# Cutting the token groups of a z product from 272, 384 and 384 columns to 272, 256, 256 and 256, with one 64-column product ahead of the first 256

## The chip, the cores and the metric

The kernel runs on one core of a Trainium2 chip, in one launch. Times are device microseconds (us). The time before is the median of three runs, 1241.5 us (1241.24 to 1242.45). A core has a matrix engine (PE, with its weight loads listed apart as PEld), a vector engine (DVE), a scalar engine (ACT), a general engine (POOL) and a queue engine (SP) that issues most transfers. Each engine works through its own list of instructions in order; semaphores tie the lists together. PE writes its sums only to PSUM, a small memory of eight banks, from which ACT or DVE must read ("evacuate") a sum before its buffer can be used again.

## The reference

One layer of a decoder over 1040 tokens (16 meta tokens and 1024 of the sequence), width 1024, float32:

```
z = h @ w_in + b_in                                  # 1024 -> 3840 columns
q, k, v, c_in, gates = split(z)                      # 512, 128, 128, 2*512, 2*1024
y_attn = sliding_window_attention(q, k, v) @ w_attn_proj
c = c_val * sigmoid(c_gate);  c = causal_dwconv(c, 31 taps)
y_conv = silu(layer_norm(c)) @ w_conv_proj
mixed = sigmoid(g_attn) * y_attn + sigmoid(g_conv) * y_conv
h = layer_norm(alpha * h + mixed @ w_out)
h = layer_norm(alpha * h + conv_ffn(h))              # 1024 -> 2*2816 -> 1024
```

The change touches the first line and the two projections that make y_attn and y_conv.

## The kernel before, in words

**Products in three terms.** Every operand of a large product is split into a high part and a low part. `product` (L294) forms, for each of eight blocks of 128 rows, high times high (L298), high times low (L302) and low times high (L303), all summed into one PSUM bank. The weights are the stationary operand (128 x 128, loaded by a LDWEIGHTS of its own ahead of each product); the tokens are the moving operand, with as many columns as the group has tokens.

**The z product.** z is computed in 30 tiles of 128 output columns. The first three (k, v and the first of q) are computed at the start, between the transposes that make h (L509 and L512), in groups `HG` = 272, 384 and 384 tokens (L54); the change leaves their groups alone. The other 27 go through `z_tile` (L313) and `z_group` (L306): for each token group a PSUM tile `ps_z` is taken from a ring of three buffers (tag "mm"), 24 products are issued, and the group's evacuation follows. Eight tiles belong to the convolution (`conv_chunk`, L640: a gate tile evacuated by ACT, L646, then a value tile evacuated by DVE into `cin`, L654, and then 31 taps on DVE over 1026 tokens, L661 and L663), three to q (evacuated by ACT at L350, with a split on DVE, L353), sixteen to the merge gates (`gate_tile`, ACT, L670, each followed by a store to `sgd` that ACT's queue issues). The q and gate tiles use `TG`, whose first group has 258 tokens in place of 272.

**Where h lies.** h0 (L255) gives the slice of h, high or low, of one block and token range; h lies in two arrays, RHO and RHC, group after group. ACT's evacuations go to staging slots in FA: `stage` (L325), five slots of 400.

**The order of work.** Each instruction has a rank; a scheduler, which simulates the engines when the kernel is built, writes each engine's list. Evacuations rank ahead of most work. While PE works on z, DVE works through the residual rows (L445), the taps, the attention's softmax, and the layer norm of the convolution; the attention's small products (scores `ps_s` L834, transposes `ps_t` L870, values `ps_o` L883) are scattered among the z products. The first product of the two meta queries is held back to a given product of the first gate tile (`ahead`).

**The projections.** After z come eight column tiles of the two projections (`branch`, from L1122): four groups `PG` of 258, 256, 256 and 256 tokens, and in each group twelve products with the attention output (OA) and twelve with the convolution (OC), into `ps_p`. After them come the product with w_out (`ps_w`), the up projection (L1552, tokens in halves of 258 and 256) and the down projection (L1696, 512 columns).

Of the kernel before, what the change touches and what calls it, by code (L numbers as in the profile page):

```python
# [31 lines left out]
KC = D // P  # L32
# [3 lines left out]
U0 = 14  # L36
# [17 lines left out]
HG = [(0, 272), (272, 656), (656, 1040)]  # L54
UG = [(0, 258), (258, 642), (642, 1026)]

PG = [(0, 258), (258, 514), (514, 770), (770, 1026)]


HW = 514  # L60
# [40 lines left out]
def tile_hybrid_layer(  # L101
# [3 lines left out]
    nc = tc.nc  # L105
# [36 lines left out]
    FA = arena.tile([P, 6144], F, name="FA")  # L142
    RHC = arena.tile([P, 8320], R, name="RHC")
    RHO = arena.tile([P, 8320], R, name="RHO")
# [22 lines left out]
    start = ExitStack()  # L167
# [85 lines left out]


    def h0(k, hl, a, b):  # L255
        g = next(g for g, x in enumerate(HG) if a < x[1])
        x, y = HG[g]
        i, n = (k % 4) * 2 + hl, y - x
        o = i * n + ((6144 if i else 0), 272, 3344)[g]
        return (RHO if k < 4 else RHC)[:, o + a - x:o + b - x]  # L260


    tc.cur_priority = RK_QKV
# [27 lines left out]

    chunks_done = []

    def product(ps, terms, behind=None):  # L294

        n = len(terms)
        for i, (ah, al, bh, bl) in enumerate(terms):
            ins = nc.tensor.matmul(ps, ah, bh, start=i == 0, stop=False)  # L298
            chunks_done.append(ins)
            if i == 0 and behind is not None:  # L300
                after(ins, behind)
            nc.tensor.matmul(ps, ah, bl, start=False, stop=False)  # L302
            last = nc.tensor.matmul(ps, al, bh, start=False, stop=i == n - 1)  # L303
        return last

    def z_group(wt, g, a, b, evac):  # L306
        hi, lo = wt
        ps = pat.tile([P, 512], F, name="ps_z", tag="mm", bufs=3)
        product(ps[:, :b - a], [(hi[:, k], lo[:, k], h0(k, 0, a, b), h0(k, 1, a, b)) for k in range(KC)])
        with rank(RK_EVAC):  # L310
            evac(g, a, b, ps[:, :b - a])

    def z_tile(fill, groups, evac, wt=None):  # L313
        wt = wt or weights([P, KC, P], fill)
        for g, (a, b) in enumerate(groups):
            z_group(wt, g, a, b, evac)

    def in_cols(m):
        return lambda raw: load(raw, w_z[m])

    TG = [(a + U0 if i == 0 else a, b) for i, (a, b) in enumerate(HG)]

    st_next = [0]

    def stage(n, lo=4104, cnt=5):  # L325
        i = st_next[0] % cnt
        st_next[0] += 1
        return FA[:, lo + i * 400:lo + i * 400 + n]

    tc.cur_priority = RK_QKV + 1000  # L330

# [272 lines left out]
    for a, b in ((0, 400), (400, J_LEN)):  # L604
        ps = pat.tile([P, 512], F, name="ps_v", tag="o" if a == 0 else "t", bufs=1 if a == 0 else 2)
# [5 lines left out]
    wt_c1 = [weights([P, KC, P], in_cols(m)) for m in (11, 7)]  # L611
# [28 lines left out]
    def conv_chunk(c):  # L640
        sig = {}

        def g_evac(g, a, b, ps):
            sig[g] = stage(b - a)

            nc.scalar.activation(sig[g], ps, AF.Tanh, bias=bcol(10 + c), scale=0.5)  # L646
            nc.scalar.activation(sig[g], sig[g], AF.Identity, bias=half_, scale=0.5)

        z_tile(in_cols(10 + c), HG, g_evac, wt_c1[0] if c == 1 else None)
        cin = cp.tile([P, 16 + T], F, name="cin", tag="cin")  # L650
        nc.vector.memset(cin[:, 0:16], 0.0)

        def v_evac2(g, a, b, ps):
            nc.vector.scalar_tensor_tensor(cin[:, 16 + a:16 + b], ps, bcol(6 + c), sig[g], OP.add, OP.mult)  # L654

        z_tile(in_cols(6 + c), HG, v_evac2, wt_c1[1] if c == 1 else None)
        with rank(RK_CONV + c * 100):
            for j in range(TAPS):
                wc = cdw[:, j * CH + c:j * CH + c + 1]
                if j == 0:  # L660
                    nc.vector.tensor_scalar(acc[c], cin[:, j:j + U], wc, cdwb(c), OP.mult, OP.add)  # L661
                else:
                    nc.vector.scalar_tensor_tensor(acc[c], cin[:, j:j + U], wc, acc[c], OP.mult, OP.add)  # L663
# [38 lines left out]
    ps = pat.tile([P, 512], F, name="ps_vm", tag="t", bufs=2)  # L702
# [4 lines left out]
    for q4 in range(2):  # L707
        ps = pat.tile([P, 512], F, name="ps_v4", tag="t", bufs=2)
        for i in range(4):
            c = NMETA + (q4 * 4 + i) * P  # L710
# [30 lines left out]
    tc.cur_priority = RK_Z - 500  # L741
    first_chunk = len(chunks_done)
    gate_tile(0)
    ahead = chunks_done[first_chunk + 2 * KC + 5]

    tc.cur_priority = RK_ATT

# [255 lines left out]
    def oo(r, hl, a, b):  # L1003
        return OA[:, place(r * 2 + hl, a, b)]
# [114 lines left out]
    for m in range(KC):  # L1119
        hi, lo = weights([P, KC, P], lambda raw: load(raw, w_ab[m]))  # L1120

        def branch(i, g, tag, bufs):  # L1122
            a, b = PG[g]
            ps = pat.tile([P, 512], F, name="ps_p", tag=tag, bufs=bufs)
            rhs = (oo, conv)[i]
            product(ps[:, :b - a], [(hi[:, 4 * i + k], lo[:, 4 * i + k], rhs(k, 0, a, b), rhs(k, 1, a, b))
                                    for k in range(4)])
            return ps[:, :b - a]

        def merge(g, psa, psb):  # L1130
            a, b = PG[g]
            n = b - a
            with rank(RK_EVAC):
                t = gslot()[:, :, :n]
                ins = load(t, dram(sgd, m * P * U + a, [[U, P], [KC * P * U, 2], [1, n]]))

                ta, tb = t[:, 0], t[:, 1]
                nc.vector.scalar_tensor_tensor(ta, ta, 1.0, psa, OP.add, OP.mult)
                nc.vector.scalar_tensor_tensor(tb, tb, 1.0, psb, OP.add, OP.mult)
                nc.vector.tensor_tensor(ta, ta, tb, OP.add)  # L1140
                if g == 0:
                    nc.scalar.mul(pair[:, m, 0:2], ta[:, 0:2], 0.5)
                v = ta[:, n - 256:].rearrange("p (t x) -> p t x", t=2)
                h = mixed2(g, m, 0)
                last_act = nc.scalar.mul(h, v, 0.5)
                nc.vector.scalar_tensor_tensor(mixed2(g, m, 1), v, 0.5, f32(h), OP.mult, OP.subtract)
            return ins, last_act

        if m < KC - 1:
            for g in range(4):  # L1150
                last_gate, last_act = merge(g, branch(0, g, "mm", 3), branch(1, g, "t", 2))
        else:
            pa = [branch(0, g, "mm", 3) if g < 3 else branch(0, g, "s", 2) for g in range(4)]
            for g in range(4):
                last_gate, last_act = merge(g, pa[g], branch(1, g, "t", 2))
        if m in (2, 3):
            raw = (FA[:, 4112:5136], OB[:, 3072:4096])[m - 2]
            load(raw, w_out_v[m + 2])
            prep_wo(m + 2, raw, last_act)
        if m < 4:  # L1160
            early.append(FA[:, W_AT[m]:W_AT[m] + 1024])
            wo_raw[m] = early[m]
            after(load(early[m], w_out_v[m]), last_gate)
        if m > 1:
            with rank(RK_PROJ + 3000):
                two_rows(m - 2)
# [261 lines left out]
    ahead = []  # L1428
# [422 lines left out]
```

## Time and profile before

| what | value |
|---|---|
| median of three runs | 1241.5 us (1241.24 to 1242.45) |
| the profiled execution | 1241.26 us, of which the span is 1239.5 us |
| granted clock of the profiled execution | 0.998 |
| z tiles of the three-group loop | PE from 56.5 to 408.0 us of the span |
| projections | PE from 408.0 to about 503 us |
| DVE busy, whole span | 1084.0 us (87%) |
| ACT busy, whole span | 580.0 us (47%) |

The span runs from the first to the last instruction that the profile shows; the execution's time has 1.76 us around it. A row of the timeline gives the start in us from the span's start, the duration in us, the engine, the line, the operation, output and inputs, their shape and count, and in brackets an idle time ahead of it with what ended it. Matmuls overlap: a row's duration is longer than the distance to the next row, and their ends are modelled. So the time that a product costs a full PE is read as the distance between starts.

### The profile page before, as it was taken

To read this page: it belongs to the slowest core of one execution; us is meant where nothing else is said; L and a number is where in the kernel's file an instruction comes from. 1 tells how busy PE (TensorE), PEld (TensorE's weight loads), DVE (VectorE), ACT (ScalarE), POOL (GpSimd) and SP (SyncE) were. 2 spreads that over 40 slices of the span, in tenths; PEclk is the share of its full clock that TensorE was granted. 3 is DMA by queue.
4 is the path that set the end of the run, shared out by engine and by line. 5 is a ranking of instruction groups with operands and counts; after the bars stand their busy time and mean duration, and the time that the engine had idled before them with its cause. 6 is when DMAs were issued, how large, how long until landed. Compare 5 with 4: busy or idle time off the path is not lost.

```text
span 1239.5 us, 21702 instructions
## 1 busy us (share of the span) xinstructions
PE 1229.4 (99%) x8540; PEld 1170.7 (94%) x8540; DVE 1084.0 (87%) x1846; ACT 580.0 (47%) x1047; POOL 12.7 (1%) x11
## 2 busy tenths in 40 slices
PE   9999999999999999999999999999999999999997
PEld 8999999999999999888999999999999998888885
DVE  7899989999978798659899999998999986995697
ACT  7532336654255323344755555455454454544330
POOL 0000000000000010000000000000000000000000
PEclk9999999999999999999999999999999999999999
DMA  7287844412255554222145555544455469987722
GB/s 283 67 300 152 199 115 107 132 37 90 75 164 154 168 165 140 102 87 85 52 171 203 205 179 213 182 176 153 162 203 194 176 239 319 391 320 290 255 85 85
DMA packets 109024, 213.08 MB, mean 172 GB/s; under 512 B 31739, under 2 KB 48683, under 8 KB 108794
## 3 DMA queue, kind: packets, MB, share of 16 engines
q1 hardware_dynamic: 93002, 200.63, 49.1%
q10 hardware_dynamic: 15920, 11.07, 2.9%
q8 instruction: 67, 1.10, 0.4%
q14 instruction: 35, 0.29, 0.1%
HBM read 150.04 MB, written 62.70 MB: 172 GB/s over the span
## 4 chain that ended last, share of the span: by engine, by line
PE 98%; DVE 1%; ACT 0%; issue 0%; DVEq 0%
PE px L1552 14%; PE py L1552 9%; PE ps_x L1696 9%; PE ps_z L302 8%; PE ps_z L298 8%; PE ps_z L303 8%; PE ps_z L1696 7%; PE pw L1552 5%; PE pz L1552 5%; PE ps_p L298 2%; PE ps_p L303 2%; PE ps_p L302 2%; PE ps_w L303 2%; PE ps_w L298 2%; PE ps_w L302 2%; PE ps_z L512 2%
## 5 line engine op out<-in xcount | busy, mean ns | idle before, releaser
L663 DVE SCALAR_TENSOR_TENSOR FA<-cin,cols,FA 128x1026 f32<-128x1026 f32 x120 | 152.1, 1278 | 0.9
L303 PE MATMUL ps_z<-RHO,wlo 128*128 128x384 f32 (+2 forms) x324 | 104.1, 321 | 0.0
L298 PE MATMUL ps_z<-RHO,whi 128*128 128x384 f32 (+2 forms) x324 | 103.9, 321 | 0.0
L302 PE MATMUL ps_z<-RHO,whi 128*128 128x384 f32 (+2 forms) x324 | 103.9, 321 | 0.0
L303 PE MATMUL ps_z<-RHC,wlo 128*128 128x384 f32 (+2 forms) x324 | 103.8, 320 | 0.0
L302 PE MATMUL ps_z<-RHC,whi 128*128 128x384 f32 (+2 forms) x324 | 103.7, 320 | 0.0
L298 PE MATMUL ps_z<-RHC,whi 128*128 128x384 f32 (+2 forms) x324 | 103.6, 320 | 0.0
L269 ACT CAST whi<-wr 128x1024 fp32r<-128x1024 f32 x37 | 38.9, 1051 | 88.7 <-PE ps_z L302 69.2
L1361 ACT CAST RHO<-wr 128x512 fp32r<-128x512 f32 x92 | 55.3, 619 | 26.2 <-DMA wr<-in_w_up_dram 12.3
L1362 DVE TENSOR_TENSOR RHO<-wr,RHO 128x512 fp32r<-128x512 f32 x92 | 61.9, 684 | 5.3 <-ACT RHO L1361 5.3
L298 PEld LDWEIGHTS ps_z<-RHO,whi 128*128 128x128 f32 x324 | 61.0, 188 | 0.1
L298 PEld LDWEIGHTS ps_z<-RHC,whi 128*128 128x128 f32 x324 | 61.1, 189 | 0.0
L303 PEld LDWEIGHTS ps_z<-RHO,wlo 128*128 128x128 f32 x324 | 61.0, 188 | 0.0
L302 PEld LDWEIGHTS ps_z<-RHO,whi 128*128 128x128 f32 x324 | 61.0, 188 | 0.0
L302 PEld LDWEIGHTS ps_z<-RHC,whi 128*128 128x128 f32 x324 | 61.0, 188 | 0.0
L303 PEld LDWEIGHTS ps_z<-RHC,wlo 128*128 128x128 f32 x324 | 60.9, 188 | 0.0
L1379 DVE TENSOR_TENSOR wr<-wr 128x512 f32<-128x512 f32 x88 | 60.1, 683 | 0.2
L272 DVE TENSOR_TENSOR wlo<-wr,whi 128x1024 fp32r<-128x1024 f32 x35 | 42.6, 1218 | 11.2 <-ACT whi L269 11.1
L670 ACT ACTIVATE FA<-ps_z,cols 128x384 f32<-128x384 f32 (+1 forms) x48 | 26.1, 543 | 47.7 <-PE ps_z L303 39.8
L1564 ACT COPY FA<-px 128x514 f32<-128x514 f32 (+2 forms) x23 | 13.1, 571 | 72.3 <-PE px L1552 72.2
L1361 ACT CAST ws<-wr 128x512 fp32r<-128x512 f32 x60 | 36.1, 618 | 17.0 <-DVE wr L1379 10.7
L1552 PE MATMUL px<-OA,RHO 128*128 128x258 f32 (+1 forms) x336 | 43.9, 279 | 0.0
(466 smaller groups left out, 3478.0 us busy)
## 6 DMA issues: line engine op xcount, KB each, us to landing
wr<-in_w_up_dram SPq DMA_DIRECT2D x44, 512.0 KB, 4.5
wr<-in_w_z_dram SPq DMA_DIRECT2D x30, 512.0 KB, 4.1
fd<-FA SPq DMA_DIRECT2D x44, 256.0 KB, 2.4
OB<-in_w_down_dram SPq DMA_DIRECT2D x19, 512.0 KB
qt<-qd SPq DMA_DIRECT2D x28, 256.0 KB, 4.2
sgd<-FA ACTq DMA_DIRECT2D x32, 192.0 KB, 3.0
td<-OB SPq DMA_DIRECT2D x12, 512.0 KB
sums<-fd SPq DMA_DIRECT2D x12, 512.0 KB, 7.0
```

Of the source, the lines that this page charges most:

```text
L269: ins = nc.scalar.copy(hi, raw)
L272: return (nc.vector if quick else nc.gpsimd).tensor_tensor(lo, raw, f32(hi), OP.subtract)
L298: ins = nc.tensor.matmul(ps, ah, bh, start=i == 0, stop=False)
L302: nc.tensor.matmul(ps, ah, bl, start=False, stop=False)
L303: last = nc.tensor.matmul(ps, al, bh, start=False, stop=i == n - 1)
L663: nc.vector.scalar_tensor_tensor(acc[c], cin[:, j:j + U], wc, acc[c], OP.mult, OP.add)
L670: nc.scalar.activation(t, ps, AF.Tanh, bias=bcol(14 + i), scale=0.5)
L1361: nc.scalar.copy(hi, src)
L1362: ins = nc.vector.tensor_tensor(lo, src, f32(hi), OP.subtract)
L1379: ins = nc.vector.tensor_tensor(*x)
L1552: ins = nc.tensor.matmul(o, x[:, ks], bmat(sub, q, hl, k), start=first and k + j == 0, stop=k == 3 and j == 2, skip_group_check=not first)
L1696: nc.tensor.matmul(banks[i], l[:, ts], r[:, ws], start=first and a and x + k == 0, stop=z and x == len(ops) - 1 and k == 2, skip_group_che ...
```

## The change

It gives the 27 z tiles of `z_tile` four groups (`ZG` = 272, 256, 256, 256; with 258 as the first for q and the gates) in place of three. In each of these tiles, ahead of the first group of 256, `product` issues one more product of 64 columns with the first block's high weights into the same PSUM tile; the next product starts the sum afresh and overwrites it. The same is done once in each of the eight column tiles of the projections, whose groups stay as they were. h is laid out anew, so that tokens 272 to 1040 of a block lie in one piece. The staging slots become seven of 286 for small groups; the five of 400 remain for the first q tile. `ahead` counts eight blocks more, so that it names the same place of the gate tile.

```diff
 PG = [(0, 258), (258, 514), (514, 770), (770, 1026)]
+ZG = [(0, 272), (272, 528), (528, 784), (784, 1040)]
...
     def h0(k, hl, a, b):
-        g = next(g for g, x in enumerate(HG) if a < x[1])
-        x, y = HG[g]
-        i, n = (k % 4) * 2 + hl, y - x
-        o = i * n + ((6144 if i else 0), 272, 3344)[g]
-        return (RHO if k < 4 else RHC)[:, o + a - x:o + b - x]
+        i = (k % 4) * 2 + hl
+        if a < 272:
+            o = i * 272 + (6144 if i > 2 else 0)
+        else:
+            o = 816 + i * 768 - 272
+        return (RHO if k < 4 else RHC)[:, o + a:o + b]
...
-    def product(ps, terms, behind=None):
+    def product(ps, terms, behind=None, lead=None):

         n = len(terms)
+        if lead is not None:
+            nc.tensor.matmul(ps[:, :64], terms[0][0], lead, start=True, stop=True)
         for i, (ah, al, bh, bl) in enumerate(terms):
...
     def z_group(wt, g, a, b, evac):
         hi, lo = wt
         ps = pat.tile([P, 512], F, name="ps_z", tag="mm", bufs=3)
-        product(ps[:, :b - a], [(hi[:, k], lo[:, k], h0(k, 0, a, b), h0(k, 1, a, b)) for k in range(KC)])
+        product(ps[:, :b - a], [(hi[:, k], lo[:, k], h0(k, 0, a, b), h0(k, 1, a, b)) for k in range(KC)],
+                lead=h0(0, 0, 0, 64) if g == 1 else None)
...
-    TG = [(a + U0 if i == 0 else a, b) for i, (a, b) in enumerate(HG)]
-
-    st_next = [0]
-
-    def stage(n, lo=4104, cnt=5):
-        i = st_next[0] % cnt
-        st_next[0] += 1
-        return FA[:, lo + i * 400:lo + i * 400 + n]
+    TG = [(a + U0 if i == 0 else a, b) for i, (a, b) in enumerate(ZG)]
+
+    st_next = [0, 0]
+
+    def stage(n):
+        big = n > 272
+        cnt, size = ((7, 286), (5, 400))[big]
+        o = 4136 + st_next[big] % cnt * size
+        st_next[big] += 1
+        return FA[:, o:o + n]
...
-        z_tile(in_cols(10 + c), HG, g_evac, wt_c1[0] if c == 1 else None)
+        z_tile(in_cols(10 + c), ZG, g_evac, wt_c1[0] if c == 1 else None)
...
-        z_tile(in_cols(6 + c), HG, v_evac2, wt_c1[1] if c == 1 else None)
+        z_tile(in_cols(6 + c), ZG, v_evac2, wt_c1[1] if c == 1 else None)
...
-    ahead = chunks_done[first_chunk + 2 * KC + 5]
+    ahead = chunks_done[first_chunk + 2 * KC + 5 + KC]
...
             product(ps[:, :b - a], [(hi[:, 4 * i + k], lo[:, 4 * i + k], rhs(k, 0, a, b), rhs(k, 1, a, b))
-                                    for k in range(4)])
+                                    for k in range(4)],
+                    lead=oo(0, 0, 0, 64) if i == 0 and g == 1 else None)
             return ps[:, :b - a]
```

## The prediction, made before the changed kernel was run

> **What bounds the kernel now.** I read the page's head and chain first, then the groups of PE instructions with their shapes, then the busy time by stage, and at last PE's timeline in the stages that the change touches.
>
> ```profile
> span 1239.5 us, 21702 instructions
> PE 1229.4 (99%) x8540; PEld 1170.7 (94%) x8540; DVE 1084.0 (87%) x1846; ACT 580.0 (47%) x1047; POOL 12.7 (1%) x11
> PE 98%; DVE 1%; ACT 0%; issue 0%; DVEq 0%
> ```
>
> PE is busy for 99% of the span and makes 98% of the chain that ends last. So what counts is the time for which each product holds PE. But DVE is close behind:
>
> ```profile
> 56.50:136.50 80.00, 80.00 (x515) 79.92 (x515) 76.28 (x91) 24.15 (x43) 0.00 (x0) 1.00 0.77 206
> 136.50:316.30 179.80, 179.80 (x1272) 178.80 (x1271) 169.94 (x352) 89.16 (x250) 0.00 (x0) 1.00 0.40 108
> 316.30:408.00 91.70, 91.70 (x590) 91.70 (x589) 77.19 (x132) 42.69 (x66) 0.00 (x0) 1.00 0.49 144
> ```
>
> The columns are the stretch, its length, and the busy time of PE, PEld, DVE, ACT and POOL, then PE's granted clock. The three stretches are z: first q and convolution tiles, then tiles with the attention among them, then gate tiles. DVE is busy for 95% of the first two. PE never sits idle, so a gain must come from cheaper products, and every wait that the change brings PE is lost in full.
>
> **What a product costs.** Durations overlap, so I take distances between starts.
>
> ```profile
> 327.54 0.28 PE L298 MATMUL ps_z<-RHO,whi 128*128 128x258 f32 x1
> 330.44 0.34 PE L298 MATMUL ps_z<-RHO,whi 128*128 128x384 f32 x1
> 338.76 0.28 PE L298 MATMUL ps_z<-RHO,whi 128*128 128x258 f32 x1
> ```
>
> This is one undisturbed gate tile: 24 products of 258 columns in 2.90 us (0.121 each), 48 of 384 in 8.32 us (0.1733 each), 11.22 us in all. The 256-column product occurs in the projections, in runs of 60 to 72, at two paces:
>
> ```profile
> 433.36 0.28 PE L298 MATMUL ps_p<-OA,whi 128*128 128x256 f32 x1
> 440.43 0.28 PE L298 MATMUL ps_p<-OA,whi 128*128 128x258 f32 x1
> ...
> 422.29 0.29 PE L298 MATMUL ps_p<-OA,whi 128*128 128x256 f32 x1
> 429.10 0.28 PE L298 MATMUL ps_p<-OA,whi 128*128 128x258 f32 x1
> ```
>
> The run at 433.36 takes 7.07 us for 60, or 0.1178 each; the one at 422.29 takes 6.81 us, or 0.1135 each. In the projections two runs (422.29 and 456.09) are fast and six slow. The up projection is fast nearly throughout:
>
> ```profile
> 821.45 1.52 PE L1552 MATMUL py<-OC,RHO 128*128 128x256 f32 x12
> 822.81 1.41 PE L1552 MATMUL px<-OA,RHO 128*128 128x256 f32 x11
> ```
>
> Twelve in 1.36 us are 0.1133 each. Three groups of 256 replace two of 384: 72 products at 0.1133 are 8.16 us against 8.32, a gain of 0.16 per tile; at 0.1178 they are 8.48, a loss of 0.16. So the pace decides the sign. What sets it? One place shows a run that follows short products:
>
> ```profile
> 597.90 0.60 PE L1331 MATMUL py<-cols,OB 128*128 128x128 f32 x4
> 598.34 0.60 PE L1331 MATMUL pz<-cols,OB 128*128 128x128 f32 x4
> 598.69 1.64 PE L1552 MATMUL pw<-RHC,RHO 128*128 128x256 f32 x12
> 600.16 1.61 PE L1552 MATMUL py<-OC,RHO 128*128 128x256 f32 x12
> 601.61 0.28 PE L1552 MATMUL px<-RHC,RHO 128*128 128x256 f32 x1
> ```
>
> Four transposes of 128 columns take 0.44 us, 0.11 each: with so few columns the spacing is no longer set by columns, but (I take it) by the weight load. From 598.34 to 600.16, four of them and twelve products of 256 take 1.82 us. Less 0.44 that is 1.38, which is twelve fast products and 0.02 for falling into step. The next twelve, after a short hitch at 600.16, take 1.45 us, or 0.1208, hitch included: slow again. So a run entered from a short product goes fast, and a small wait makes it slow. A 64-column product is such a short one; I take it that the lead does what it is placed for, from this one instance.
>
> **The change part by part.**
>
> *The lead.* Nearest row to it is a single product of 8 columns among products of 384:
>
> ```profile
> 182.40 0.34 PE L302 MATMUL ps_z<-RHO,whi 128*128 128x384 f32 x1
> 182.58 0.17 PE L798 MATMUL ps_o<-p,va 80*128 80x8 f32 x1
> 182.61 0.43 PE L303 MATMUL ps_z<-RHO,wlo 128*128 128x384 f32 x1
> 182.88 0.33 PE L298 MATMUL ps_z<-RHO,whi 128*128 128x384 f32 x1
> ```
>
> Two products of 384 and the small one take 0.48 us; less 0.347 the small one costs 0.13. Bounds: 0.11 (a transpose) and 0.15 (this with 0.02 for falling into step). I take 0.13. There are 27 leads in z and 8 in the projections.
>
> *An undisturbed tile* then takes 2.90 + 0.13 + 8.16 = 11.19 us, a gain of 0.03. Over 27 tiles: **-0.8**.
>
> *Tiles with the attention among them.* Twelve tiles lie between 136.5 and 316.3. In the built order of the changed kernel 58 stretches of 256 begin behind an attention product. A stretch of 256 pays 0.02 to fall into step, one of 384 about 0.01:
>
> ```profile
> 178.58 1.04 PE L790 MATMUL ps_t<-cols,s 128*16 128x128 f32 x8
> 179.63 0.34 PE L298 MATMUL ps_z<-RHO,whi 128*128 128x384 f32 x1
> ```
>
> (1.05 us for eight transposes at 0.109 and one product of 384 at 0.173.) So 58 x 0.01 = **+0.6**, bounds 0 and 1.2. And some stretches will be slow, since most begin behind transposes or scores but some behind a wait or the 256-column `ps_o`. All twelve slow would cost 12 x 72 x 0.0045 = 3.9; none, nothing. I take a quarter: **+1.0**.
>
> *A new wait at the second tile.* A tile now takes four turns of the three PSUM buffers, so its last group needs the buffer of its first. In the value tile of conv chunk 1 that buffer is read late:
>
> ```profile
> 68.38 0.29 PE L298 MATMUL ps_z<-RHO,whi 128*128 128x272 f32 x1
> 71.37 0.34 PE L298 MATMUL ps_z<-RHO,whi 128*128 128x384 f32 x1
> ...
> 74.34 1.21 DVE L272 TENSOR_TENSOR wlo<-wr,whi 128x1024 fp32r<-128x1024 f32 x1
> 75.47 2.34 DVE L445 TENSOR_TENSOR OB<-OB,gb 128x1024 f32<-128x1024 f32 x2
> 77.75 1.01 DVE L654 SCALAR_TENSOR_TENSOR cin<-ps_z,cols,FA 128x272 f32<-128x272 f32 x2
> ...
> 79.70 0.29 PE L298 MATMUL ps_z<-RHO,whi 128*128 128x272 f32 x1
> ```
>
> DVE runs without a gap up to the evacuation at 77.75 and frees the buffer at about 78.2. Before, its next user starts at 79.70. In the built order DVE has the same instructions ahead of that evacuation, so 78.2 stays. PE now reaches the fourth group at 71.37 + 0.13 + 48 x 0.1133 = 76.9, and waits 1.3, with the wake-up **+1.4**. Behind it on PE stands everything. Bounds: 0 (if DVE gets there earlier) and 1.4.
>
> *Evacuations.*
>
> ```profile
> L654 DVE SCALAR_TENSOR_TENSOR cin<-ps_z,cols,FA 128x384 f32<-128x384 f32 x8 | 4.9, 611 | 2.3 <-PE ps_z L303 2.3
> L670 ACT ACTIVATE FA<-ps_z,cols 128x384 f32<-128x384 f32 x16 | 9.2, 578 | 17.9 <-PE ps_z L303 10.1 <-DMA sgd<-FA 7.4 <-ACT FA L670 0.5
> ...
> 346.63 0.33 ACTq L116 DMA_DIRECT2D sgd<-FA  x1
> ```
>
> A tile has one more, estimated at three of some 465 ns for two of about 600. On DVE that is some 0.2 in each of the four value tiles and as much for the splits of three q tiles; on ACT, with 0.33 for the issue of one more store, some 0.5 in each of the others. Stores of the gates and writes of q grow in number by a third, not in bytes. All this lies beside PE, and I cost it at nothing. It has cover as long as attention operands come early: in
>
> ```profile
> 200.62 0.69 DVE L874 TENSOR_TENSOR pl<-ps_t,ph 80x512 fp32r<-80x512 f32 x1
> 205.01 0.28 PE L883 MATMUL ps_o<-pl,va 80*128 80x256 f32 x1
> ```
>
> DVE ends 3.7 us ahead of PE's use. The built order puts fewer taps and fewer z products ahead of each attention step, by my sums of the rows' durations up to 5 us less for DVE than for PE; the margin and the wait above take that up. Without them PE would wait 1 to 2 us more.
>
> *Projections.* Six of eight runs are slow, 348 products in all (72, four of 60, 36). At 0.0043 that is -1.5; eight leads cost +1.04. Together **-0.5**.
>
> *The new layout of h* moves no work: the same slices are written and read.
>
> **Sum:** -0.8 + 0.6 + 1.0 + 1.4 - 0.5 = +1.7. On the profiled execution's 1241.26 us (span 1239.5 and 1.76 around it) that is 1242.96; the median of the runs lies 0.24 higher, so **1243.2 us**. Faster or slower is what differs by over 0.2%, 2.5 us, which is about what a measurement can tell from no change.
>
> **The rivals.**
>
> *The pace is not to be had in z (slower).* Products of 258 and 384 lie on a line: 0.0523 us for 126 columns, so 0.107 for 258 and a fixed 0.014. By it 256 columns cost 0.120, and the measured 0.1178 is near. If the lead doesn't help, or a first wait undoes it, each z tile takes 2.90 + 0.13 + 8.48 = 11.51, +0.29, 7.8 for 27; the projections' eight leads and the loss of the two quick stretches (132 x 0.0043) give +1.6; the wait is then 1.1. In all +10.5: 1252. It decides as soon as some three z tiles more than I count run slow (0.32 each, past the 2.5 us). Against it stand the fast up projection and the run behind the transposes. The Trainium skill speaks for it too: TensorE: Matmul & The Clock Gate, section Back-to-back issue gap, gives a warm product N/2.4 + 2.5 ns, a fixed part each, so that three of 256 never beat two of 384; by it z would lose 0.17 per tile with a lead of 0.11, and the kernel would come to about 1248. The rows disagree in size: 0.1133 and 0.1178 in place of 0.109, 0.1733 in place of 0.1625. It shares this rival's chance.
>
> *Evacuation and attention come late.* Groups of 256 leave two turns of 2.72 us, not 4.16, to free a buffer. In the layer norm of the convolution ACT reads a 258-column sum at 366.95, some 1.3 us after PE began the next group at 365.67:
>
> ```profile
> 365.67 0.34 PE L298 MATMUL ps_z<-RHO,whi 128*128 128x384 f32 x1
> 366.95 0.46 ACT L670 ACTIVATE FA<-ps_z,cols 128x258 f32<-128x258 f32 x1
> 363.52 1.28 ACT L670 ACT_TABLE_LOAD   x1
> ```
>
> and the built order has one more table load (1.28 us) on ACT there. If this and the attention each cost 1.5 to 2 us, the time is 1246.5.
>
> *All covers hold.* Leads of 0.11, no slow stretches, no falling into step, no wait: 1243.2 - 0.7 - 0.6 - 1.0 - 1.4 = 1239.5. The arithmetic hardly reaches 0.2% faster.
>
> **How the numbers follow.** The forecast gets 0.52 (0.44 within 0.2%, 0.08 over it), the missing pace 0.15, late evacuations 0.20, the covers 0.13 (0.08 faster, 0.05 within). So faster 0.08, same 0.49, slower 0.43. The range goes from the covers' 1239.5 to 1250, which takes in the upper bounds (all attention tiles slow +2.9, leads +0.7, entries +0.6, late evacuation +2 or so) and leaves out the missing pace and a little below.
>
> **What would show it.** Starts of 256-column products in undisturbed z tiles 0.113 apart (right) or 0.118 (the first rival); a lead's pair of starts with 0.11 to 0.15 more; a PE wait of 1.4 us near 77 ended by DVE line 661; projections of 11.0 us a tile. Wrong would be the sum if PE waits elsewhere, or the attention tiles run slow throughout.

## The result, and the profile after

| kernel | median | runs | against the kernel before |
|---|---|---|---|
| before | 1241.76 us (1241.24 to 1243.12) | 7 | |
| after | 1245.76 us (1245.49 to 1247.11) | 7 | 1.0031, 95% interval 1.0020 to 1.0042 |

The change makes the kernel 4.0 us, or 0.31%, slower. The forecast was 1243.2 us, 1.7 above the three runs that stood on record before (median 1241.5): the sign was right, the loss was more than twice as large. By the prediction's own line of 0.2% this is slower, to which it gave a chance of 0.43, and 0.49 to the same.

The head of the page after, with its chain:

```profile
span 1244.4 us, 23138 instructions
PE 1230.4 (99%) x9223; PEld 1172.0 (94%) x9223; DVE 1087.5 (87%) x1853; ACT 588.6 (47%) x1078; POOL 12.8 (1%) x11
PE 92%; DVE 4%; DMA 2%; ACT 2%; issue 1%; SPq 0%; DVEq 0%; ACTq 0%
```

PE is busy 1.0 us longer, but the span is 4.9 us longer. So most of the loss is time in which PE stands still. The chain says so too: 98% PE before, 92% now, with DMA, DVE and ACT in it. PE's waits in the profile after (engine, line, what it waited for: us in total, times, longest):

```profile
PE ps_s L841 <- DMA qt<-qd: 2.3, 1, 2.3
PE ps_w L543 <- DVE sel L1094: 1.1, 1, 1.1
PE ps_h L469 <- DVE xn L433: 0.9, 1, 0.9
PE ps_z L302 <- DVE cin L661: 0.8, 1, 0.8
PE pw L1560 <- DVE OA L1245: 0.4, 1, 0.4
PE ps_z L516 <- ACT FA L475: 0.3, 1, 0.3
PE ps_z L302 <- ACT FA L677: 0.2, 1, 0.2
```

The rows for `sel`, `OA` and line 516 (1.1, 0.4 and 0.3 us) stand in the same view of the kernel before too, under its own line numbers. New are 2.3 us for a load of q ahead of the first attention scores, 0.8 us at the value tile of conv chunk 1, 0.2 for ACT, and 0.9 at the very start. By stage, as distances between starts of products in the two traces:

| stage | before | after | difference |
|---|---|---|---|
| start of the span to the last transpose ahead of z | 56.5 us | 57.1 us | +0.65 |
| from there to the first scores | 84.3 | 89.5 | +5.3 |
| first scores to the last attention product | 171.0 | 150.7 | -20.3 |
| from there to the first projection product | 96.3 | 116.5 | +20.2 |
| first to last projection product | 94.6 | 93.8 | -0.8 |
| from there to the last product | 728.2 | 728.3 | 0.0 |

The third and fourth rows only shift z products from one side of the attention's end to the other. The first row is not the change's doing: the kernel below with the lead in the projections alone, which has the start of the kernel before, shows the same kind of wait there, and longer:

```profile
PE ps_h L464 <- DVE xn L428: 1.6, 1, 1.6
```

So the two profiled executions differ by some 0.6 us at the start, and the medians (+4.0) are the better measure of the rest. The two long new waits lie ahead of the first scores. Not all of the loss does: the changed kernel has eleven products of 256, 1.25 us, more ahead of the scores than the kernel before, so that at equal work, and without the waits, z's products take about 1.0 us more ahead of the scores and 1.0 us more behind them.

### The profile page after: what moved, and what is told of

Its sections match the earlier page's. It is cut to its first block, busy times and chain, and to the rows that moved or that the text cites. A ratio compares the mean times of both kernels' runs of the same rounds, so it can differ in the third digit from the quotient of the medians.

```text
span 1244.4 us, 23138 instructions
## 1 busy us (share of the span) xinstructions
PE 1230.4 (99%) x9223; PEld 1172.0 (94%) x9223; DVE 1087.5 (87%) x1853; ACT 588.6 (47%) x1078; POOL 12.8 (1%) x11
## 4 chain that ended last, share of the span: by engine, by line
PE 92%; DVE 4%; DMA 2%; ACT 2%; issue 1%; SPq 0%; DVEq 0%; ACTq 0%
PE px L1560 14%; PE py L1560 9%; PE ps_x L1704 9%; PE ps_z L1704 7%; PE ps_z L302 7%; PE ps_z L306 7%; PE ps_z L307 7%; PE pw L1560 5%; PE pz L1560 5%; PE ps_p L302 2%; PE ps_p L306 2%; PE ps_p L307 2%; PE ps_w L307 2%; PE ps_w L302 2%; PE ps_w L306 2%; PE ps_z L519 2%
## 5 line engine op out<-in xcount | busy, mean ns | idle before, releaser
L302 PE MATMUL ps_z<-RHO,whi 128*128 128x256 f32 (+2 forms) x432 | 124.1, 287 | 0.9 <-DVE cin L661 0.8
L302 PE MATMUL ps_z<-RHC,whi 128*128 128x256 f32 (+2 forms) x432 | 121.3, 281 | 0.0
L306 PE MATMUL ps_z<-RHC,whi 128*128 128x256 f32 (+2 forms) x432 | 121.2, 281 | 0.0
L307 PE MATMUL ps_z<-RHC,wlo 128*128 128x256 f32 (+2 forms) x432 | 121.1, 280 | 0.0
L306 PE MATMUL ps_z<-RHO,whi 128*128 128x256 f32 (+2 forms) x432 | 121.0, 280 | 0.0
L307 PE MATMUL ps_z<-RHO,wlo 128*128 128x256 f32 (+2 forms) x432 | 120.8, 280 | 0.0
L302 PEld LDWEIGHTS ps_z<-RHO,whi 128*128 128x128 f32 x432 | 81.3, 188 | 1.4 <-DVE cin L661 1.0
L306 PEld LDWEIGHTS ps_z<-RHO,whi 128*128 128x128 f32 x432 | 81.5, 189 | 0.0
L306 PEld LDWEIGHTS ps_z<-RHC,whi 128*128 128x128 f32 x432 | 81.4, 188 | 0.0
L302 PEld LDWEIGHTS ps_z<-RHC,whi 128*128 128x128 f32 x432 | 81.3, 188 | 0.0
L307 PEld LDWEIGHTS ps_z<-RHC,wlo 128*128 128x128 f32 x432 | 81.2, 188 | 0.0
L307 PEld LDWEIGHTS ps_z<-RHO,wlo 128*128 128x128 f32 x432 | 81.2, 188 | 0.0
L271 ACT CAST whi<-wr 128x1024 fp32r<-128x1024 f32 x37 | 38.8, 1049 | 67.4 <-PE ps_z L306 47.2
L677 ACT ACTIVATE FA<-ps_z,cols 128x258 f32<-128x258 f32 (+1 forms) x64 | 30.2, 472 | 69.1 <-PE ps_z L307 56.2
```

Of the source, the lines that this page charges most:

```text
L271: ins = nc.scalar.copy(hi, raw)
L677: nc.scalar.activation(t, ps, AF.Tanh, bias=bcol(14 + i), scale=0.5)
```

## The wait that was not foreseen

SP's list around the first loads of q, before and then after (start, duration, what is issued, count; `x3` is a group of three issues with the gaps between them):

```profile
128.30 0.35 SPq L112 DMA_DIRECT2D wr<-in_w_z_dram  x1
129.27 0.33 SPq L112 DMA_DIRECT2D qd<-qsh  x1
129.97 2.34 SPq L112 DMA_DIRECT2D qd<-qsl  x3
134.60 1.78 SPq L112 DMA_DIRECT2D qt<-qd  x3
```

```profile
131.90 0.39 SPq L113 DMA_DIRECT2D wr<-in_w_z_dram  x1
132.38 2.96 SPq L113 DMA_DIRECT2D qd<-qsl  x3
140.01 0.50 SPq L113 DMA_DIRECT2D qt<-qd  x1
140.56 0.58 SPq L113 DMA_DIRECT2D qd<-qsl  x1
141.20 1.15 SPq L113 DMA_DIRECT2D qt<-qd  x2
```

q goes through DRAM: DVE makes its low half (`qsl`), SP writes it (`qd<-qsl`), and when it has landed SP loads it back in the attention's order (`qt<-qd`). Before, the loads begin 2.3 us after the end of the third write's issue (132.31 to 134.60); after, 4.7 (135.34 to 140.01). Besides, a further write, of the next group of 256, now stands between the first load and the second. The pieces of the chain after, from DVE's split to the scores:

```profile
134.18 0.35 DVE qsl L360
...
134.91 4.91 DMA qd<-qsl
...
141.20 5.33 DMA qt<-qd
...
146.67 1.09 PE ps_s L841 x8
```

The write takes 4.9 us to land, the load 5.3, and PE waits for the second load. Its last z product ahead of the scores starts at 144.12; the scores start at 146.67. The same chain lies in the kernel before, where the loads start at 134.60 and the scores at 140.74 without a wait: it was hidden. The trace also records when the last piece of a transfer has landed, so the links can be set side by side:

| link | before | after |
|---|---|---|
| DVE's split of the first group of the last q tile starts | 131.06 us | 134.09 us |
| its write, from issue to landing | 131.88 to 134.46 | 134.91 to 139.82 |
| the second load, from issue to landing | 135.15 to 139.46 | 141.20 to 146.53 |
| PE is free for the scores | 140.74 | 144.39 |

Before, the load landed 1.3 us ahead of the scores. After, it lands 7.1 us later than before and PE is free only 3.7 us later, which uses up the 1.3 and leaves the wait. Of the 7.1 us 3.0 stand in the split, 2.3 in the write, 0.6 between the issues of the first load and the second, where the further write stands, and 1.0 in the second load.

## The experiments

The kernel before, run beside each of these on the same chip, had medians of 1241.4 to 1242.2 us; ratios are against it.

### Scores later

```diff
+    scores_behind = chunks_done[first_chunk + 3 * KC - 1]
...
+                        if i + g + u + h + j == 0:
+                            after(ins, scores_behind)
```

> The changed kernel with the first score product of the attention ordered behind the end of the second group of its gate tile, 25 products of 256 later on PE than before. Theory: in the changed kernel PE sits idle 2.3 us at 144.4 until the load of q has landed (146.67), a wait that the kernel before does not have; 25 products take 2.8 us and cover it, so the wait goes and the time is 1245.8 - 2.3 = 1243.5 us; the attention ends some 100 us ahead of the last gate tile, so its later start costs nothing. Rival: what bounds the attention is DVE, and a later start only moves the wait into its later steps: 1245.3 us or more.

Measured 1243.56 us, 1.0015 (1.0005 to 1.0024): 2.2 us less than the changed kernel, as the theory had it. In its trace PE has no wait for q, and its other waits are those of the changed kernel. So the wait for q is a loss of its own, worth 2.2 us, and it doesn't come back in the attention.

### What makes q late: the load ahead of it, or the split

In the first kernel the load of the weights of gate tile 2 is put behind the write:

```diff
+                q_put[r, g, hl] = put(dram(qd, q_at(i) + (hl * 4 + r) * HD, ...
...
+        if o == 2:
+            after(last_fill[-1], q_put[3, 0, 1])
```

> The changed kernel with one load moved on SP's queue: the 512 KB of weights for gate tile 2, issued at 131.91 between the writes of q, are ordered behind the last write of q that the first scores need (134.92 there). Theory 1: that write lands late (its reader on SP goes on at 139.85, 4.9 us after the issue; 2.3 us in the kernel before) because the weights' data move ahead of it on the same queue from 133.0 to 135.5. Then it lands some 2 us earlier here and PE's wait for q (2.3 us in the changed kernel) falls to 0.5 us or less. Theory 2: q is late because DVE makes its low halves late, and the queue doesn't matter: the wait stays within 0.5 us of 2.3.

In the second the halves of q have three buffers (the first q tile takes others):

```diff
-    qsp = qsp_stack.enter_context(tc.tile_pool(name="qsp", bufs=2, side="right", reuse_waits="tile"))
+    qsp = qsp_stack.enter_context(tc.tile_pool(name="qsp", bufs=3, side="right", reuse_waits="tile"))
...
+            h, l = (sp.tile([P, 384], R, name=n, tag=n, bufs=2)[:, :b - a] if r == 0 else
+                    qsp.tile([P, 258], R, name=n, tag=n)[:, :b - a] for n in ("qsh", "qsl"))
```

> The changed kernel with three buffers in place of two for the high and for the low halves of q, 258 columns wide in place of 400. Theory 1 (as for the load behind): the wait of PE for q comes from the weights ahead on the queue, and DVE's waits of 2.4 us for the buffers of the low halves, which go here, have no part in it: PE still waits 2 us or more. Theory 2: those waits put DVE back, and with it the low halves of the last q tile; without them PE's wait for q falls to 0.5 us or less.

Measured once each, so the reading goes by the traces and not by the times: 1243.68 us with the load behind, and no PE wait for q; 1244.38 us with three buffers, and a wait of

```profile
PE ps_s L842 <- DMA qt<-qd: 0.6, 1, 0.6
```

SP's list in the one and in the other:

```profile
131.72 4.26 SPq L113 DMA_DIRECT2D qd<-qsl  x3
136.03 0.50 SPq L113 DMA_DIRECT2D wr<-in_w_z_dram  x1
136.63 0.39 SPq L113 DMA_DIRECT2D qd<-qsl  x1
138.33 1.79 SPq L113 DMA_DIRECT2D qt<-qd  x3
```

```profile
131.43 0.38 SPq L113 DMA_DIRECT2D wr<-in_w_z_dram  x1
131.90 3.46 SPq L113 DMA_DIRECT2D qd<-qsl  x4
138.90 1.14 SPq L113 DMA_DIRECT2D qt<-qd  x2
```

I had put the two causes up as alternatives. The first passes its test with the load behind and fails with three buffers; the second fails with the load behind and all but passes with three buffers (0.6 us where it asked for 0.5 or less). So both are links of one chain. With the weights out of the way the loads follow the third write by 2.3 us, as in the kernel before, and the first starts at 138.33 in place of 140.01. With three buffers it starts at 138.90; DVE's waits for the landing of earlier writes are 1.0 us in place of 2.4. In both, the second load follows the first at once, since no write stands between them: that too takes time off. So the chain got longer in three places: groups of 256 come every 2.7 us and two buffers no longer cover a landing of 4.9; the weights stand closer ahead of the write (their last piece lands 1.6 us after the write's issue, 0.2 in the kernel before); and one more write stands among the loads. The built order moved too: against the changed kernel PE has eight products of 256 more ahead of the scores with the load behind (0.9 us), which covers some, and five fewer with three buffers (0.6 us), about what is left of the wait there. So how the 2.3 us divide among the three these two runs don't settle. The Trainium skill's page DMA: Bandwidth & Descriptors, section Queues, rings and completion order, says that each DMA engine takes the descriptors of one queue in ring order; the traces agree: loads that wait for the write start 4.7 us after the end of its issue with 512 KB of weights ahead of it on SP's queue, and 2.3 us with the weights behind.

### The convolution in its old groups

```diff
-        z_tile(in_cols(10 + c), ZG, g_evac, wt_c1[0] if c == 1 else None)
+        z_tile(in_cols(10 + c), HG, g_evac, wt_c1[0] if c == 1 else None)
...
-        z_tile(in_cols(6 + c), ZG, v_evac2, wt_c1[1] if c == 1 else None)
+        z_tile(in_cols(6 + c), HG, v_evac2, wt_c1[1] if c == 1 else None)
```

> The changed kernel with the eight convolution tiles back in groups of 272, 384 and 384 (no lead there); q, gates and projections as changed. Theory A: the PSUM wait of 0.9 us in the value tile of conv chunk 1 goes, and in the first four conv tiles 192 products of 384 (33.3 us) stand in place of four leads and 288 products of 256, three tiles of four at the slow pace (33.8 us): -1.4 us; the other four about even. q comes earlier with PE, so the wait for q stays at 2.3: 1244.4 us. Theory B: the wait for q is set by DVE's backlog and SP's queue, not by when PE ends q; then what PE gains ahead of it is lost in it, the wait grows to 3.7 us and the time stays 1245.8 us.

Measured 1241.77 us, 1.0002 (0.9992 to 1.0011). (In this kernel the staging slots of two sizes overlap, so that some of the convolution's gate values are overwritten ahead of their use; the instructions are those that the text says.) Both theories missed: 4.0 us went, and neither the wait of the value tile nor that for q is left. The first loads of q start at 136.56 and 137.1 there, one right behind the other, and the scores at 141.45; so the order of SP's list moved with the convolution's groups, which neither theory had thought of. The next kernel takes the same thing in smaller steps.

### Chunk 1 in its old groups, and the scores later

Only the two tiles of chunk 1 go back, with staging slots of one size for them, together with the edit of the later scores:

```diff
+    CG = {1: HG, 0: ZG, 2: ZG, 3: ZG}
...
+        z_tile(in_cols(10 + c), CG[c], g_evac, wt_c1[0] if c == 1 else None)
...
+        z_tile(in_cols(6 + c), CG[c], v_evac2, wt_c1[1] if c == 1 else None)
```

> The changed kernel with the two tiles of conv chunk 1 back in groups of 272, 384 and 384, and the first scores ordered behind the second group of their gate tile. Theory: what the change costs is a sum of parts that can be taken away one by one. The later scores alone gave 1243.6; the PSUM wait of the value tile is worth 0.9 us more, and 96 products of 384 (16.65 us) for two leads and 144 products of 256, mostly slow (16.95), 0.3: 1242.4 us, with no PE wait over 0.5 us between 57 and 410. Rival: DVE is as far behind as before, and what PE gains at 77 us it waits for at the next evacuation or at the scores: 1243.5 us.

Measured 1241.92 us, 1.0002 (0.9993 to 1.0011), near the theory's 1242.4 and far from the rival's 1243.5. Of the new waits in z only 0.2 us for ACT is left. So the two tiles of chunk 1 cost 1.6 us against the kernel with the later scores (1.4 by the two traces): 0.8 is the wait for the PSUM buffer, which stands in the changed kernel's trace where the prediction put it (a row of PE, then one of DVE),

```profile
78.92 0.39 PE L302 MATMUL ps_z<-RHO,whi 128*128 128x256 f32 x1 [0.76 <-DVE cin L661]
78.38 0.87 DVE L661 SCALAR_TENSOR_TENSOR cin<-ps_z,cols,FA 128x272 f32<-128x272 f32 x2
```

and the rest, 0.7 by the traces, is slow products, to which the next three go.

### What the lead does

```diff
-                lead=h0(0, 0, 0, 64) if g == 1 else None)
+                lead=None)
...
-                    lead=oo(0, 0, 0, 64) if i == 0 and g == 1 else None)
+                    lead=None)
```

> The changed kernel without any 64-column product, in z and in the projections. Theory: the leading product is what brings most runs of 256 into the quick pace (0.1133 us a product; slow 0.1178). In the changed kernel's trace 1495 of the 1944 z products stand in quick runs and the slow pace costs 1.65 us in all; a lead with the first product behind it takes 0.229 us, 0.116 more than a product. Without leads 35 x 0.116 = 4.1 us go, and if all 1944 run slow 1944 x 0.0045 = 8.7 come in place of 1.65, and 1.6 in the projections: 1245.8 - 4.1 + 7.1 + 1.6 = 1250.4 us, with starts 0.118 apart in the quiet gate tiles. Rival: the pace is set by something else and the leads only cost: 1241.7 us, quiet gate tiles still 0.113 apart.

Measured 1246.39 us, 1.0038 (1.0025 to 1.0052): 0.6 us above the changed kernel, which the intervals don't tell from nothing, and between the two theories. Of the 1944 products of 256 in z, those in stretches with starts more than 0.116 apart on average rise from some 440 to some 1200; the rest stay quick without a lead, many of them behind the attention's products. A quiet gate tile without and with the lead (here and below the rows at which the number of columns changes):

```profile
319.10 0.28 PE L302 MATMUL ps_z<-RHO,whi 128*128 128x258 f32 x1
321.98 0.28 PE L302 MATMUL ps_z<-RHO,whi 128*128 128x256 f32 x1
...
330.46 0.28 PE L302 MATMUL ps_z<-RHO,whi 128*128 128x258 f32 x1
```

```profile
310.81 0.28 PE L302 MATMUL ps_z<-RHO,whi 128*128 128x258 f32 x1
313.68 0.19 PE L300 MATMUL ps_z<-RHO,whi 128*128 128x64 f32 x1
313.70 0.36 PE L302 MATMUL ps_z<-RHO,whi 128*128 128x256 f32 x1
...
321.97 0.28 PE L302 MATMUL ps_z<-RHO,whi 128*128 128x258 f32 x1
```

From one first product to the next it takes 11.36 us without and 11.16 with; the kernel before takes 11.22. So the lead works in the quiet tiles. But over the whole of z it hardly pays: less PE's waits there, z takes 353.8 us without leads (356.5 less 2.7) and 353.5 with (356.8 less 3.3). What the theory missed besides: without leads the wait for q is only 0.2 us, while ACT's evacuations cost PE 1.5 in place of 0.2.

In the changed kernel the lead fails in three of the first four tiles, which have a first group of 272:

```profile
96.53 0.20 PE L300 MATMUL ps_z<-RHO,whi 128*128 128x64 f32 x1
...
105.12 0.28 PE L302 MATMUL ps_z<-RHO,whi 128*128 128x258 f32 x1
```

The lead and 72 products take 8.59 us there and 8.29 in the quiet tile; two groups of 384 took 8.32. So I changed the lead's length, to 128 and to 16 columns:

```diff
-            nc.tensor.matmul(ps[:, :64], terms[0][0], lead, start=True, stop=True)
+            nc.tensor.matmul(ps[:, :128], terms[0][0], lead, start=True, stop=True)
...
```

> The changed kernel with leads of 128 columns in place of 64. Theory: what the lead does is to have the first product of 256 enter behind a product that is bound by its weight load, so 128 columns (0.108 to 0.112 us a product in the transposes) act as 64 do: the same pattern of starts, quick quiet gate tiles (0.113), slow tiles behind the groups of 272 columns. Rival: what counts is the moment at which the run starts against some beat of the weight loads, so that another length of lead makes other tiles quick and slow; then the tiles behind 272 columns or the quiet gate tiles change pace.

> The changed kernel with leads of 16 columns in place of 64. Theory: as for 128 columns, the same tiles quick and slow, and the lead with the first product behind it still takes 0.23 us, since it is the weight load that is paid. Rival: the pace follows the moment of the start, and other tiles are quick and slow; the cost of a lead changes with its columns.

Measured once each: 1248.73 us with 128 columns, 1250.34 with 16. With 16, two quiet gate tiles in a row:

```profile
315.13 0.17 PE L300 MATMUL ps_z<-RHO,whi 128*128 128x16 f32 x1
315.16 0.36 PE L302 MATMUL ps_z<-RHO,whi 128*128 128x256 f32 x1
323.42 0.28 PE L302 MATMUL ps_z<-RHO,whi 128*128 128x258 f32 x1
326.29 0.17 PE L300 MATMUL ps_z<-RHO,whi 128*128 128x16 f32 x1
326.31 0.36 PE L302 MATMUL ps_z<-RHO,whi 128*128 128x256 f32 x1
334.88 0.28 PE L302 MATMUL ps_z<-RHO,whi 128*128 128x258 f32 x1
```

The same 72 products take 8.26 us in one tile and 8.57 in the next, and so on, nearly always in turn: a quick tile is followed by a slow one and a slow one by a quick one. With 128 columns it is the same in the quiet tiles, while the four tiles behind 272 columns are all quick. The projections, first to last product, take 95.5 us with either, 93.8 with 64 columns and 94.6 without leads. So the theory falls (a short product as such doesn't make a run quick), and the rival fits better: the pace hangs on what ran ahead. What passes it on, a moment of the start or some state of PE, these runs don't show. 64 columns are the length with which a quick tile is followed by a quick one here.

### The projections alone, and with the quiet gates

The kernel before with the lead in the projections only:

```diff
+        if lead is not None:
+            nc.tensor.matmul(ps[:, :64], terms[0][0], lead, start=True, stop=True)
...
-                                    for k in range(4)])
+                                    for k in range(4)],
+                    lead=oo(0, 0, 0, 64) if i == 0 and g == 1 else None)
```

> The kernel before with the 64-column product in the projections alone (8 leads), z as before. Theory: the projections' quick pace is the lead's own doing and does not hang on z: from first to last projection product 93.8 us in place of 94.6, so 1241.8 - 0.8 = 1241.0 us. Rival: the pace there came with what stands ahead of the projections (z's new groups) and the leads cost 8 x 0.12 = 0.9 us for nothing: 1242.7 us.

Measured 1240.60 us, 0.9990 (0.9981 to 1.0000); the second time, beside the kernel that follows,

> The kernel before with the lead in the projections alone, once more, beside the one with the quiet gate tiles. Theory: 0.8 us under the kernel before, 1240.8 us. Rival: the 1.0 us seen at first was mostly the chip's own spread, and the gain is under 0.4 us: 1241.3 us.

1240.62 us, 0.9990 (0.9982 to 0.9999). The projections take 93.8 us in place of 94.6, whichever of the groups z has. This is the one version that beats both kernels, by 1.0 us in both sessions, at the edge of what the intervals can tell; 0.8 of it stands in the projections of the trace. The first lead of it and the 72 products behind, up to the next tile:

```profile
411.25 0.19 PE L298 MATMUL ps_p<-OA,whi 128*128 128x64 f32 x1
...
419.54 0.28 PE L300 MATMUL ps_p<-OA,whi 128*128 128x258 f32 x1
```

That is 8.29 us; the prediction's run of 72 at the slow pace would take 8.48 without a lead.

Then the same in the quiet gate tiles, with all other z tiles in their old groups (against the changed kernel):

```diff
...
-        z_tile(in_cols(14 + i), TG, gate_evac)
+        z_tile(in_cols(14 + i), TG if i >= 8 else QG, gate_evac)
...
```

> The kernel before with the changed groups and the lead in the gate tiles 8 to 15 alone, which lie behind the attention, and with the projections' leads. Theory: a quiet gate tile gains 0.06 us (11.16 in place of 11.22), eight of them 0.5, less some 0.1 for those that the layer norm's sums cut; with 0.8 from the projections 1241.6 - 1.2 = 1240.4 us. Rival: the evacuations of three tiles at the layer norm come late (PE waited 0.4 us for ACT there in the changed kernel) and eat the gain: 1240.9 us, no better than the projections alone.

Measured 1243.64 us, 1.0015 (1.0006 to 1.0024), 3.2 us off the theory and worse than its rival. Its trace shows one new wait in z,

```profile
383.15 0.38 PE L302 MATMUL ps_z<-RHO,whi 128*128 128x256 f32 x1 [1.60 <-ACT FA L678]
```

at the layer norm of the convolution, where ACT has its table loads (the late evacuation that the prediction's second rival put there). A second new wait, 1.0 us for ACT in the up projection, lengthens nothing: from the last projection product to the last product of all it takes 728.2 us, as in the kernel before. And there is a surprise: the products of 384 behind a first group of 258 start 0.1767 apart, not 0.1734 as in the kernel before. They are the same products. But this kernel has the changed layout of h.

### The layout of h alone

```diff
-        g = next(g for g, x in enumerate(HG) if a < x[1])
-        x, y = HG[g]
-        i, n = (k % 4) * 2 + hl, y - x
-        o = i * n + ((6144 if i else 0), 272, 3344)[g]
-        return (RHO if k < 4 else RHC)[:, o + a - x:o + b - x]
+        i = (k % 4) * 2 + hl
+        if a < 272:
+            o = i * 272 + (6144 if i > 2 else 0)
+        else:
+            o = 816 + i * 768 - 272
+        return (RHO if k < 4 else RHC)[:, o + a:o + b]
```

> The kernel before with the changed kernel's layout of h alone: the same instructions in the same order on every engine, only the places of h's slices in the two buffers differ (in the kernel with the quiet gate tiles, which has this layout too, 384-column products behind 258 columns start 0.1767 apart, in the kernel before 0.1734). Theory: the layout alone sets this, so that tiles behind the convolution's run slow: some 15 tiles of 48 products with 0.0033 each are 2.4 us: 1244.0 us. Rival: the slow 384 there came with what else was new, and the layout, as the prediction had it, costs nothing: 1241.6 us.

Measured 1244.24 us, 1.0018 (1.0008 to 1.0027): with the same instructions in the same order, 2.0 us more (2.8 in z by the two traces). A quiet gate tile of it:

```profile
318.26 0.28 PE L299 MATMUL ps_z<-RHO,whi 128*128 128x258 f32 x1
321.15 0.34 PE L299 MATMUL ps_z<-RHO,whi 128*128 128x384 f32 x1
329.63 0.28 PE L299 MATMUL ps_z<-RHO,whi 128*128 128x258 f32 x1
```

48 products take 8.48 us. In the tile of the kernel before that the prediction quotes they take 8.32 (330.44 to 338.76). By the traces some 800 of its 1296 products of 384 in z run at the slower pace, and some 20 in the kernel before. So where the moving operand lies in SBUF is enough to change the pace. Which property of the places does it stays open, and so does what the layout costs the changed kernel itself: its groups of 256 cross the slices of the old layout, so they can't be run with it.

## Why the prediction was right or wrong, point by point

The sum had +1.7; the medians show +4.0. The runs divide it: 2.2 for q (scores later), 1.6 for the two tiles of chunk 1 (the step from there to the kernel with both), -0.8 in the projections, and by difference 1.0 for the rest of z. Each of these medians is good to about 1 us, by the intervals. The two profiles give the same picture in other cuts: waits 3.3 us where the sum had 1.4, z's products +2.0 (353.5 for 351.5) where it had +0.8, the projections -0.8 where it had -0.5.

- **Evacuations "at nothing": this step failed.** The prediction wrote that writes of q grow in number, not in bytes, that all this lies beside PE, and saw a cover in DVE's lead over the attention's value products. It looked at the attention's later steps and not at its first load. The cover there was 1.3 us, and the chain got 3.4 us longer against PE: in the kernel before the load lands at 139.46 and the scores come at 140.74; after, PE is free at 144.39 and the load lands at 146.53. Taking the wait away gave 2.2 us, about the 2.3 that the sum was short. That the two match so well is partly luck, since the other terms were off as well and nearly cancel.
- **The new wait at the second tile (+1.4): right in place and cause, 0.8 in size.** DVE began the evacuation at 78.38 (77.75 before) and freed the buffer at 78.9 (78.2 forecast); PE came to the fourth group at 78.2 and not at 76.9. The span's start, 0.65 later, moved both; slow products ahead of it, which the forecast had as quick, took up the rest.
- **An undisturbed tile (-0.03, in all -0.8): right for the quiet ones, wrong for the convolution's.** The quiet tiles gain 0.06 (11.16 for 11.22). But the four tiles ahead of q were counted among the undisturbed, and three of them ran slow: without the wait the four take 47.2 us for 46.3, where the sum had a gain of 0.1.
- **Slow products in the attention (+1.0): right in size, by a guess.** In the changed kernel's trace some 440 of 1944 products stand in slow stretches: some 230 of them among the attention (at 0.0045 each 1.0 us) and some 170 in the first four tiles (0.8), which had no such term. The prediction took a quarter of the attention's products without a reason for the quarter, so that it came out is luck.
- **"A run entered from a short product goes fast, and a small wait makes it slow": wrong.** It was read from one instance. Leads of 16 and 128 columns give quick and slow tiles nearly in turn. The conclusion, that 64 columns make quiet tiles quick, held by luck: by the length that the change happens to have.
- **The projections (-0.5): right, -0.8.** A lead with the first product takes 0.23 us, 0.12 more than a product (0.13 forecast), and the runs behind a lead are quick in all eight tiles.
- **"The new layout of h moves no work": true, and no reason to cost it at nothing.** It made some 800 products slower in the kernel before. The changed kernel has no product of 384 in these tiles, so the sum didn't suffer from this in the way shown; whether its products of 256 suffer is open.
- **The rivals.** The missing pace (1252) did not come. The late evacuations (1246.5) came nearest in time, 0.7 us off where the forecast is 2.6 off, and in kind: a wait of the attention of 2.3 us and one of ACT of 0.2; but the attention's came through SP and DRAM, not through DVE's backlog in the softmax. The formula of the Trainium skill (TensorE: Matmul & The Clock Gate, section Back-to-back issue gap) has one gap for 256 columns and one for 384, and the section gives it for a product on its own, not for a stream of weight loads and products as here; the traces have two of each, 0.1133 and 0.1178, 0.1734 and 0.1767.

## What to carry to other kernels

Where a change cuts a stage into more pieces, follow each piece to the first reader of what it makes, through DRAM too, and compare the landing with the time at which that reader comes: bytes and busy shares say nothing of a chain that was hidden with 1.3 us to spare. With PE at 99%, what remains of a finer cut is the pace of the products, and that hangs on what ran ahead and on where the operands lie; so measure an edit of this kind stage by stage, alone, and keep only the part that pays (here the projections).

## What the runs showed of the hardware that was not expected

- The same fp32 products run at two steady paces: 256 columns 0.1133 or 0.1178 us apart, 384 columns 0.1734 or 0.1767. A run without a wait keeps its pace to its end, up to 72 products.
- The pace of a quiet tile follows from what ran ahead of it: with leads of 16 columns quick and slow tiles nearly alternate (8.26 and 8.57 us), with 64 they stay quick. Why isn't shown.
- The addresses of the moving operand alone change it: the same instructions in the same order, 8.48 us in place of 8.32 for 48 products, 2.0 us over the kernel.
- A write of 128 KB in pieces of 256 bytes took 4.9 us from issue to landing behind a 512 KB load issued 3.0 us ahead of it on the same queue, and 2.6 in the kernel before, where that load was issued 3.6 us ahead; loads that wait for the write followed the end of its issue by 2.3 us when the 512 KB stood behind it.
